# One encoder layer on one Trainium2 core: a new head, another start of the attention, one more early block in each feed-forward product, and sums moved by a turn

## The chip, the cores and the metric

The kernel runs on one core of one Trainium2 chip. The time is the device time of one execution in microseconds (us), lower is better. The core has five engines that are followed here: PE (TensorE: matrix products and transposes), DVE (VectorE), ACT (ScalarE), POOL (GpSimd) and SP (SyncE, which in this kernel only issues DMA transfers; POOL issues most of the others). Each engine works through its own list of instructions in order; between engines there are semaphores.

## The reference, cut to what matters

One layer over a sequence of 1024 rows of 1024 numbers, all in fp32:

```
h = swiglu(rmsnorm(x, ffn1_pre_g), w_gate, w_up, w_down)     # 1024 -> 2816 -> 1024
x = x + 0.5 * rmsnorm(h, ffn1_post_g)
h = rmsnorm(x, mix_pre_g);  q, k, v = h @ w_qkv              # 16 heads of 64
o_na  = neighbourhood_attention(first 8 heads, rel_bias)     # 16 x 64 grid, softmax
o_dil = dilated_mixture(last 8 heads, t5_bias)               # 3 windowed softmaxes, merged
x = x + rmsnorm([rmsnorm(o_na) | rmsnorm(o_dil)] @ w_out, mix_post_g)
x = x + 0.5 * rmsnorm(swiglu(rmsnorm(x, ffn2_pre_g), ...), ffn2_post_g)

rmsnorm(x, g) = x * rsqrt(mean(x*x) + 1e-6) * g
swiglu(x)     = (silu(x @ w_gate) * (x @ w_up)) @ w_down
```

## The kernel before

**Numbers.** Every fp32 operand is split in a high part (ACT: a cast to fp32r, `hi`) and the rest (DVE: a subtraction, `lo`). A product is three matrix products, hi·hi (L268), lo·hi (L269), hi·lo (L270), in one PSUM bank.

**Strassen.** Large products are done with one level of Strassen-Winograd: seven block products instead of eight. The operand (the normalised rows, transposed) exists in seven forms (A11, A12, A22 and sums S1 to S4), the weights too. `PairGemm` does the gate and up projections in 22 blocks of 128 columns: block b takes one 512 KB load of each of the two weight matrices, and seven **chains** of 12 matmuls 128x512, one chain for each form. `run` goes through the blocks: u (L491), v (L499), c22 (L520) and c21 (L528) are the additions on DVE that put the chains together, and c21 belongs to a last chain (A22) that is held back and runs in the next block. A chain that goes on in a bank waits for the addition that reads the bank ahead of it. The weight sums of the next block (L453 to L455) and the splits (L362 on ACT, L363 on DVE) are spread over the block.

**Early blocks.** The operand of a sub-layer is made from rows that arrive in eight tiles of 128 rows. The first four tiles give A11 and A12. So `ahead` runs the A11 and A12 chains of the first `early` blocks before the rest of the operand exists, and keeps their sum in DRAM (L438); `plan` gives each of these turns some steps (norm, transposes of one tile, sums of the operand). In `run`, an early block has five chains and loads its kept sum (L487). Before, there are 9 early blocks in the first feed-forward product (FFN1), 8 in the q/k product, 11 in the second (FFN2). The gated product of a block goes to `sink`: L568 to L587, in which every odd block adds four sums for the pair. Near the end of each gate phase the down projection's weights are summed as well (L333 to L335).

**Head.** The start of the program: two tiles of x are loaded, the norm weights come as a row broadcast to 128 partitions (512 KB, on POOL's queue), ACT squares the rows, DVE makes the root in 12 small operations on 128x2 (L143 to L154), then scales each tile (L217), PE transposes it (L176), ACT and DVE split it (L177, L178). Then the A11 chains of blocks 0 and 1 run by halves of 256 columns. From the first turn of `ahead` on, each block has A11 and A12 chains, and the tiles 4 to 7 are normed and transposed beside them.

**q/k product.** A planned `ahead` of 8 turns, whose turn 0 ends the sums and makes the norm of tiles 6 and 7 and transposes tile 5, then value passes, then `run` over 8 blocks; block 7's last chain ends it. Each block's q and k of one pair of heads are split, written to DRAM by POOL (L893 to L911) and read back as `st`. Two plan entries load the first heads of the attention (`load_head`: g, va and vb, 13 DMAs for the first), at turns 5 and 7.

**Attention, first head.** A head of the dilated group is worked in units of two blocks of 128 queries: scores on PE (L1035), maximum with bias on DVE (L935), exponentials on ACT (L940), four transposes on PE (L946), a copy (L951), values on PE (L1047). The order of units is a small pipeline: PE does the scores of units ahead of the transposes of the one before. The q of the first head is rearranged by residue on ACT (L917, 128x1024), that of later heads on POOL.

Of the kernel before, what the change touches and what calls it, by code (L numbers as in the profile page):

```python
# [19 lines left out]
P, T = 128, 512  # L20
# [319 lines left out]
class PairGemm:  # L340
# [137 lines left out]
    def run(self, final=None):  # L478
# [3 lines left out]
        for b in range(self.n):  # L482
# [48 lines left out]
            c.tick()  # L531
        last()


class GatePairs:
# [7 lines left out]
    def first(self, b, ps, keep, s1=None):  # L543
        c, nc = self.c, self.c.nc
        sg = c.sp.tile([P, T], F32, tag="s1", name="sg") if keep else self.tile()
# [306 lines left out]
class QKPairs:  # L852
# [15 lines left out]
    def last(self, b, q, k):  # L868
        self.put(b, 0, 1, q)
        self.put(b, 1, 1, k)  # L870

    def put(self, b, kind, h, x):
        c, nc = self.c, self.c.nc
        p = QK_ORDER[b]
        e = c.sp.tile([P, 2, T], F32R, tag="qk", name="qk", bufs=c.qkbufs)
# [44 lines left out]
def q_by_residue(c, copy, st):  # L920
    q = c.op.tile([P, SEQ], F32R, tag="q", name="q")
    by_residue(copy, q, st[:, 0])
    return q
# [53 lines left out]
class DilPair:  # L977


    def __init__(self, c, p, then):  # L980

        self.c, self.p, self.pi, self.then = c, p, p - NP, then
# [7 lines left out]
    def outputs(self):  # L990
        c = self.c
        self.oa = c.op.tile([P, 8, VW], F32, tag="oa", name="oa")
        self.sa = c.op.tile([P, 8, 2], F32, tag="sa", name="sa")
        self.ob = c.op.tile([P, 8, RW], F32, tag="ob", name="ob")

    def head(self, hd, st, q, g, late, parts=(1, 0)):
        for part in parts:
            for quad in range(2):
# [6 lines left out]
    def unit(self, hd, st, q, g, part, quad, un, po):  # L1005
# [5 lines left out]
        def scores():  # L1011
            ps = c.pss.tile([P, 2, 256], F32, tag="s", name="sp")
            s = c.pp.tile([P, 2, 256], F32, tag="s", name="s")
            pb = s if part else c.op.tile([P, 2, 256], F32, tag="pb", name="pb", bufs=4)
# [218 lines left out]
def layer(tc, a, out):  # L1233
    nc = tc.nc
    c = Ctx(tc)
    with ExitStack() as ctx:
# [80 lines left out]
        def ffn(which, op, prep, pg, get, turns, sums, more, post, pre, src, dst, begin=None,  # L1317
# [8 lines left out]
            if begin:  # L1326
                left_pool(e)
                pg.start()
# [95 lines left out]
        with ExitStack() as order:  # L1424
# [9 lines left out]
            load((0, 1), (nc.sync, nc.scalar))  # L1434
            op0 = Operand(c, load_gain(c, a["ffn1_pre_g"], "pre"), 0)

            def begin(pg):
                load((2, 3), (nc.scalar, nc.sync))

                def drain():  # L1440
                    while c.sums:
                        c.sums.popleft()()

                def norm(*ts):
                    op0.scale(*n[ts])
                    drain()
                def junk():
                    return c.xp.tile([P, D], F32, tag="s", name="junk", bufs=2)
                n = {(0, 1): op0.squares([0, 1], [xs[0], xs[1]], junk())}
                norm(0, 1)  # L1450
                pg.split_left(0)
                n[2, 3] = op0.squares([2, 3], [xs[2], xs[3]], junk())
                op0.one(0)
                op0.one(1)
                pg.split_left(1)
                acc, s1 = [pg.bank() for _ in range(2)], []
                for b in range(2):
                    pg.mm(acc[b], pg.w[b], 0, A11, cols=slice(0, 256))
                op0.one(0)
                norm(2, 3)  # L1460
                op0.one(2)
                op0.one(3)
                for b in range(2):
                    pg.mm(acc[b], pg.w[b], 0, A11, cols=slice(256, 512))
                    s1.append(pg.save(b, acc[b]))
                    if b:
                        op0.one(1)
                load((4, 5), (nc.gpsimd, nc.gpsimd))
                op0.one(2)
                op0.one(3)  # L1470
# [30 lines left out]
            op, fin, hs, prep = ffn(1, op0, prep, gate_pairs(1, op0, a["wg1"], a["wu1"], 9), get1,  # L1501
# [271 lines left out]
```

## Time and profile before

| | us |
|---|---|
| median of 3 runs | 1900.07 (1899.72 to 1904.05) |
| the profiled execution | 1899.15 |
| its span in the trace | 1897.0 |
| PE busy in the span | 1842.2 (97%) |
| DVE busy | 1316.3 (69%) |
| ACT busy | 794.9 (42%) |
| POOL busy | 320.7 (17%) |

The span is what the trace covers; around it lie 2.15 us that no engine's instruction shows. PE is at work for 97% of the span, so a time is read from this profile by asking where PE stands still, or runs at a lower clock, and what it waits for there. Durations stand in the rows as nanoseconds or microseconds of one instruction; in rows of the timeline the first number is the start in us, the second how long the row's instructions took together, and the bracket says how long the engine was idle before and what released it.

### The profile page before, as it was taken

What the parts mean: (1) busy time and instruction counts of PE and PEld (TensorE: products, weight loads), DVE (VectorE), ACT (ScalarE), POOL (GpSimd) and SP (SyncE); (2) the same over time, 40 slices, a digit from 0 to 9 for tenths busy, and PEclk for the clock granted to TensorE, in tenths of its full rate; (3) what the DMA queues carried; (4) which work ended last, traced back from release to release, by engine and by line L of the source; (5) the groups of instructions that cost most, each with busy time, mean ns of one, the idle gap of its engine ahead of it and who ended that gap; (6) DMA issues with size and microseconds to landing.
All of it is one profiled execution on the core that took longest, in us unless ns stands there. A gap on an engine that the chain in (4) does not pass through costs nothing.

```text
span 1897.0 us, 25061 instructions
## 1 busy us (share of the span) xinstructions
PE 1842.2 (97%) x9044; PEld 1538.3 (81%) x9044; DVE 1316.3 (69%) x2207; ACT 794.9 (42%) x1285; POOL 320.7 (17%) x519
## 2 busy tenths in 40 slices
PE   5999999999999999999999999999999999999997
PEld 4778788888887887888799987877887888888886
DVE  5778777765655977568566775786878777655557
ACT  4522233333444545324477765453222333344342
POOL 1122122211000022222342310121111111110000
PEclk8999999999999999999999999999999999999999
DMA  6655667664986756656974642484456656576563
GB/s 236 219 195 180 219 204 237 234 235 139 348 297 214 273 170 235 234 161 201 314 262 137 219 157 89 165 311 161 159 191 215 223 190 223 197 276 209 195 230 134
DMA packets 162748, 402.52 MB, mean 212 GB/s; under 512 B 17664, under 2 KB 34272, under 8 KB 160576
## 3 DMA queue, kind: packets, MB, share of 16 engines
q1 hardware_dynamic: 113312, 225.67, 35.6%
q0 software_dynamic: 48448, 173.15, 25.7%
q10 hardware_dynamic: 864, 2.10, 0.3%
q8 instruction: 71, 1.16, 0.2%
q14 instruction: 53, 0.43, 0.1%
HBM read 275.89 MB, written 130.03 MB: 214 GB/s over the span
## 4 chain that ended last, share of the span: by engine, by line
PE 84%; DVE 6%; DMA 4%; issue 3%; ACT 2%; POOL 0%; SPq 0%; DVEq 0%; ACTq 0%; POOLq 0%
PE mmp L268 16%; PE mmp L270 16%; PE mmp L269 16%; PE accp L269 8%; PE accp L268 8%; PE accp L270 8%; PE po L1047 3%; PE ptp L946 2%; PE sp L1035 2%; PE trp L176 1%; PE po L1168 1%; PE sp L1155 1%; DMA tsv<-tr 1%; DMA sgd<-sg 1%; DMA gain<-in_ffn_pre_g_dram 0%
## 5 line engine op out<-in xcount | busy, mean ns | idle before, releaser
L268 PE MATMUL mmp<-x,whi 128*128 128x512 f32 (+1 forms) x1432 | 565.8, 395 | 6.5 <-DVE v L499 4.2
L270 PE MATMUL mmp<-x,wlo 128*128 128x512 f32 (+1 forms) x1432 | 561.2, 392 | 1.7 <-DVE wlo L363 1.7
L269 PE MATMUL mmp<-x,whi 128*128 128x512 f32 (+1 forms) x1432 | 560.7, 392 | 0.5 <-DVE x L178 0.2
L268 PEld LDWEIGHTS mmp<-x,whi 128*128 128x128 f32 x1432 | 271.1, 189 | 67.2 <-issue 6.5
L270 PEld LDWEIGHTS mmp<-x,wlo 128*128 128x128 f32 x1432 | 271.0, 189 | 61.0 <-DVE wlo L363 2.4
L269 PEld LDWEIGHTS mmp<-x,whi 128*128 128x128 f32 x1432 | 271.3, 189 | 58.0 <-DVE x L178 1.4
L638 DVE TENSOR_TENSOR pw<-praw,pw 128x1024 fp32r<-128x1024 f32 (+1 forms) x182 | 199.0, 1138 | 124.6 <-ACT pw L637 122.7
L362 ACT CAST whi<-wraw 128x1024 fp32r<-128x1024 f32 x128 | 134.0, 1051 | 325.7 <-PE mmp L269 257.2
L637 ACT CAST pw<-praw 128x1024 fp32r<-128x1024 f32 (+1 forms) x182 | 168.9, 983 | 206.3 <-PE accp L270 158.6
L269 PE MATMUL accp<-pw 128*128 128x512 f32 x600 | 233.7, 390 | 1.0 <-DVE pw L638 1.0
L268 PE MATMUL accp<-pw 128*128 128x512 f32 x600 | 234.3, 391 | 0.0
L270 PE MATMUL accp<-pw 128*128 128x512 f32 x600 | 233.6, 389 | 0.0
L363 DVE TENSOR_TENSOR wlo<-wraw,whi 128x1024 fp32r<-128x1024 f32 x128 | 156.3, 1223 | 22.3 <-ACT whi L362 22.3
L269 PEld LDWEIGHTS accp<-pw 128*128 128x128 f32 x600 | 112.7, 188 | 24.7 <-DVE pw L638 1.9
L268 PEld LDWEIGHTS accp<-pw 128*128 128x128 f32 x600 | 112.6, 188 | 23.7 <-DVE hb L709 0.2
L270 PEld LDWEIGHTS accp<-pw 128*128 128x128 f32 x600 | 112.6, 188 | 23.6
L570 POOL DMA_DIRECT2D g<-sg x44 | 24.1, 548 | 445.0 <-DVE sg L563 291.7
L381 ACT COPY s<-mmp 128x512 f32<-128x512 f32 x52 | 30.5, 586 | 143.0 <-PE mmp L270 135.5
L178 DVE TENSOR_TENSOR x<-trp,x 128x512 fp32r<-128x512 f32 x84 | 57.3, 687 | 38.7 <-ACT x L177 38.6
L528 DVE TENSOR_TENSOR c<-mmp,u 128x512 f32<-128x512 f32 x52 | 35.8, 688 | 66.3 <-PE mmp L270 66.3
L177 ACT CAST x<-trp 128x512 fp32r<-128x512 f32 x84 | 48.8, 586 | 53.1 <-PE trp L176 52.7
L453 DVE TENSOR_TENSOR wraw<-wraw 128x1024 f32<-128x1024 f32 x52 | 63.5, 1221 | 0.8
(246 smaller groups left out, 2742.6 us busy)
## 6 DMA issues: line engine op xcount, KB each, us to landing
praw<-g SPq DMA_DIRECT2D x70, 512.0 KB
wraw<-in_wg_dram SPq DMA_DIRECT2D x44, 512.0 KB
wraw<-in_wu_dram SPq DMA_DIRECT2D x44, 512.0 KB
tr<-in_wd_dram SPq DMA_DIRECT2D x44, 512.0 KB
g<-sg POOLq DMA_DIRECT2D x88, 256.0 KB, 4.4
ts<-tr POOLq DMA_DIRECT2D x22, 1024.0 KB, 4.9
praw<-ts SPq DMA_DIRECT2D x88, 256.0 KB
praw<-in_wd_dram SPq DMA_DIRECT2D x66, 256.0 KB
```

The costliest lines, as they stand in the source:

```text
L177: nc.scalar.copy(hi, ps)
L178: nc.vector.tensor_sub(lo, ps, hi.bitcast(F32))
L268: nc.tensor.matmul(out, ahi, bhi, start=start, stop=False, skip_group_check=go_on)
L269: nc.tensor.matmul(out, ahi, blo, start=False, stop=False, skip_group_check=go_on)
L270: nc.tensor.matmul(out, alo, bhi, start=False, stop=stop, skip_group_check=go_on)
L362: nc.scalar.copy(hi, raw)
L363: nc.vector.tensor_sub(lo, raw, hi.bitcast(F32))
L453: nc.vector.tensor_sub(r[:, 0:2], r[:, 1:3], r[:, 0:2])
L637: nc.scalar.copy(w[side][:, 0, :m], raw[:, :m])
L638: nc.vector.tensor_sub(w[side][:, 1, :m], raw[:, :m], w[side][:, 0, :m].bitcast(F32))
L946: c.nc.tensor.transpose(self.tps[:, j, :], self.probs[:, j * P:(j + 1) * P], c.ident)
L1047: nc.tensor.matmul(po[0][:, un * 2 + j], u.pt[:, 2 * j + t, :], rhs, start=t == 0, stop=t == 1)
```

## The change

1. **Head.** `begin` is written by hand for all engines. The norm weights come as one row of 4 KB and are spread over the partitions by two matmuls with a row of ones (L1480). Tile 0 and 2 are squared on ACT, tile 1 and 3 on DVE. The root is one Sqrt on ACT and five small DVE operations (L1497 to L1501). Tiles are scaled in halves of 512 columns, weights are loaded and split in halves of 256 KB, x2 and x3 change queues. The A11 chains of three blocks, not two, run there, those of block 0 and 1 by halves, and all eight transposes of the halves of the first four tiles stand between them.
2. **Early blocks.** 10 in FFN1 (the tiles 4 to 7 one turn later in the plan, and the norm of 4 and 5 after ACT's work of its turn), 12 in FFN2.
3. **q/k product.** In `ahead`, the sums and the norm of tiles 6 and 7 and the transposes of tile 5 go from turn 0 to turn 1. In `run`, `load_head` comes at turns 4 and 5, the rearranging of the first head's q (now on POOL) and of its bias at turn 6.
4. **Attention.** The scores of the first two units stand ahead of the last chain of the q/k product, in banks of that product's own pool (`ahead=` of `run`, `begin` of the head, `early` of the unit). The last block's second q/k write is held back (`held`) and done between the first units of the attention.

The core of the diff:

```diff
@@ PairGemm.run
-    def run(self, final=None):
+    def run(self, final=None, ahead=None):
...
             c.tick()
+        if ahead:
+            ahead()
         last()
@@ QKPairs
     def last(self, b, q, k):
-        self.put(b, 0, 1, q)
-        self.put(b, 1, 1, k)
-
-    def put(self, b, kind, h, x):
+        es = [self.tile() for _ in range(2)]
+        for kind, x in enumerate((q, k)):
+            put = lambda kind=kind, x=x: self.put(b, kind, 1, x, es[kind])
+            if b == len(QK_ORDER) - 1:
+                self.c.held.append(put)
+            else:
+                put()
@@ DilPair
+    def begin(self, st, g):
+        self.sa = self.c.small.tile([P, 8, 2], F32, tag="sa", name="sa", bufs=1)
+        po = []
+        for un in range(2):
+            self.c.unit(self.unit(0, st, None, g, 0, 0, un, po, True))
...
         def scores():
-            ps = c.pss.tile([P, 2, 256], F32, tag="s", name="sp")
...
+            if early:
+                ps, s, pb = [pool.tile([P, T], F32, tag=t, name="se" + t).rearrange("p (a b) -> p a b", a=2)
+                             for pool, t in ((c.psm, "mm"), (c.sp, "s1"), (c.sp, "v"))]
+            else:
+                ps = c.pss.tile([P, 2, 256], F32, tag="s", name="sp")
@@ the head
+                nc.scalar.dma_start(row[:1, :D], a["ffn1_pre_g"])
+                load((0, 1), (nc.sync, nc.scalar))
+                fetch(0, 0)
+                load((3, 2), (nc.scalar, nc.sync))
+                for b, i in ((1, 0), (2, 0), (0, 1), (1, 1), (2, 1)):
+                    fetch(b, i)
...
+                for g, ps in enumerate(spread):
+                    nc.tensor.matmul(ps, row[:1, D:], row[:1, g * T:g * T + T], start=True, stop=True)
...
+                def root(t):
+                    x = ss[:, t:t + 2]
+                    q, h, y, e = [c.small.tile([P, 4], F32, tag=n, name=n)[:, :2] for n in ("q0", "v", "y", "e")]
+                    nc.scalar.activation(q, x, AF.Sqrt, bias=eps[:, 0:1], scale=1.0 / D)
+                    nc.vector.tensor_scalar(h, x, -0.5 / D, -0.5 * EPS, op0=ALU.mult, op1=ALU.add)
+                    nc.vector.reciprocal(y, q)
+                    nc.vector.tensor_mul(e, y, h)
+                    nc.vector.tensor_mul(e, e, y)
+                    nc.vector.scalar_tensor_tensor(y, e, 1.5, y, op0=ALU.add, op1=ALU.mult)
...
+                square(0)
+                square_here(1)
+                root(0)
+                nc.scalar.copy(op0.gain[:, :T], spread[0])
+                whigh(0, 0)
+                scale(0, 0)
+                scale(1, 0)
+                turn(0, 0)
+                turn(1, 0)
+                square(2)
+                square_here(3)
+                high(0, 0)
...
+                products(0, (0, 1, 2), first)
...
+                products(2, (2,), every)
+                low(3, 1)
...
@@ the plans
-    ... gate_pairs(1, op0, a["wg1"], a["wu1"], 9), get1,
-        {0: [F(4, 5), L(6, 7)], 2: [U(4)], 3: [F(6, 7), U(5)], 5: [U(6)], 6: [U(7)]},
+    ... gate_pairs(1, op0, a["wg1"], a["wu1"], 10), get1,
+        {0: [lambda: c.behind(F(4, 5), ACT), L(6, 7)], 3: [U(4)], 4: [F(6, 7), U(5)], 6: [U(6)], 7: [U(7)]},
-            plan(8, {0: [A(6, 7), U(5)], 3: [U(6)], 5: [U(7)]})
+            plan(8, {1: [A(6, 7), U(5)], 3: [U(6)], 5: [U(7)]})
-            plan(8, {5: [lambda: queued(load_head)], 7: [lambda: queued(load_head), lambda: queued(first_bias)]})
-            pg.run()
+            plan(8, {4: [lambda: queued(load_head)], 5: [lambda: queued(load_head)],
+                     6: [lambda: queued(first_q), lambda: queued(first_bias)]})
+            c.held, qs = [], deque()
+            pg.run(ahead=ahead)
...
-            pg = gate_pairs(3, op, a["wg2"], a["wu2"], 11)
+            pg = gate_pairs(3, op, a["wg2"], a["wu2"], 12)
```

Three places show how instructions move. In these rows a line of the kernel, an operation, what it writes and reads, and its size stand in the order of one engine; the changed kernel's line numbers are some 10 (later 156) higher for the same code.

PE at the start of the program, before (`trp` is the bank of transposes, `mmp` a bank of products, `xn` a scaled tile):

```order
L176 MATMUL trp<-ident,xn 128x128 x8
L268 MATMUL mmp<-x_155,whi 128x256
L269 MATMUL mmp<-x_156,whi 128x256
L270 MATMUL mmp<-x_155,wlo 128x256
L268 MATMUL mmp<-x_155,whi 128x256
L269 MATMUL mmp<-x_156,whi 128x256
```

and now:

```order
L1480 MATMUL mmp<-row 128x512 x2
L1517 MATMUL trp<-ident,xn 128x128 x8
L1542 MATMUL mmp<-x_149,whi 128x256 x4
L1542 MATMUL mmp<-x_150,whi 128x256 x4
L1542 MATMUL mmp<-x_149,wlo 128x256 x4
L1542 MATMUL mmp<-x_149,whi 128x256 x4
L1517 MATMUL trp<-ident,xn 128x128 x4
L1542 MATMUL mmp<-x_150,whi 128x256 x4
L1517 MATMUL trp<-ident,xn 128x128 x4
L1542 MATMUL mmp<-x_149,wlo 128x256 x4
L1542 MATMUL mmp<-x_149,whi 128x256 x4
L1542 MATMUL mmp<-x_150,whi 128x256 x4
```

The two matmuls that spread the norm weights are first; the transposes of tiles 2 and 3 (rows of x4) stand between the products of block 1 instead of behind both blocks' first halves.

SP in the q/k product's run, from the weight load of one block on, before (`wraw` are a block's weights, `s` is its kept sum, `g`, `va` and `vb` belong to a head of the attention):

```order
L355 DMA wraw<-in_wqk_dram 128x2x512
L356 DMA wraw<-in_wqk_dram 128x1024
L487 DMA s_7316<-s1d 128x512
L355 DMA wraw<-in_wqk_dram 128x2x512
L356 DMA wraw<-in_wqk_dram 128x1024
L973 DMA g<-gab_68 128x384
L973 DMA g<-gab_69 128x384
L961 DMA va<-v_88 128x7x130
L961 DMA va<-v_88 128x2x130 x2
L965 DMA vb<-v_88 128x1x130 x8
L973 DMA g<-gab_68 128x384
L973 DMA g<-gab_69 128x384
```

and now:

```order
L355 DMA wraw<-in_wqk_dram 128x2x512
L356 DMA wraw<-in_wqk_dram 128x1024
L983 DMA g<-gab_68 128x384
L983 DMA g<-gab_69 128x384
L971 DMA va<-v_88 128x7x130
L971 DMA va<-v_88 128x2x130 x2
L975 DMA vb<-v_88 128x1x130 x8
L487 DMA s_7355<-s1d 128x512
L355 DMA wraw<-in_wqk_dram 128x2x512
L356 DMA wraw<-in_wqk_dram 128x1024
L983 DMA g<-gab_68 128x384
L983 DMA g<-gab_69 128x384
```

Before, the 13 transfers of the first `load_head` (g, va, vb) stand behind the last block's weights (the second pair of `wraw` rows); now the same 13 stand behind those of the block before, and the last block's kept sum and weights stand behind the 13.

PE at the end of the q/k product, before (`sp` are scores, `ptp` transposes of the probabilities, `po` products with the values):

```order
L269 MATMUL mmp<-x_5409,whi 128x512
L270 MATMUL mmp<-x_5408,wlo 128x512
L1035 MATMUL sp<-st 128x256 x12
L946 MATMUL ptp<-ident,pb 128x128 x4
L1035 MATMUL sp<-st 128x256 x4
L946 MATMUL ptp<-ident,pb 128x128 x4
L1035 MATMUL sp<-st,q 128x256 x4
L1047 MATMUL po<-va,pt 128x65 x4
```

and now (`semm` are scores in a bank of the product's pool):

```order
L269 MATMUL mmp<-x_5431,whi 128x512
L270 MATMUL mmp<-x_5430,wlo 128x512
L1056 MATMUL semm<-st 128x256 x8
L268 MATMUL mmp<-x_5432,whi 128x512
...
L270 MATMUL mmp<-x_5432,wlo 128x512
L1056 MATMUL sp<-st 128x256 x4
L956 MATMUL ptp<-ident,sev 128x128 x4
L1056 MATMUL sp<-st 128x256 x4
L956 MATMUL ptp<-ident,sev 128x128 x4
L1056 MATMUL sp<-st,q 128x256 x4
L1068 MATMUL po<-va,pt 128x65 x4
```

The scores of the first two units (x8) have moved ahead of the last chain of 12 matmuls. On DVE the same place reads before (k, c: the last additions of the product; L890 the split of q and k, L935 the maximum of a unit's block):

```order
L865 TENSOR_TENSOR k<-mmp,u_7331 128x512
L890 TENSOR_TENSOR qk<-k,qk 128x512
L528 TENSOR_TENSOR c_7428<-mmp,u_7331 128x512
L890 TENSOR_TENSOR qk<-c_7389,qk 128x512
L890 TENSOR_TENSOR qk<-qk 128x512
L935 ISA s,sa<-sp,g 128x256
```

and now:

```order
L867 TENSOR_TENSOR k<-mmp,u_7370 128x512
L945 ISA ses_7453,sa<-semm,g 128x256
L945 ISA sa 128x1
L945 ISA ses_7453,sa<-semm,g 128x256
L945 ISA sa 128x1
L900 TENSOR_TENSOR qk<-k,qk 128x512
L945 ISA ses_7462,sa<-semm,g 128x256
L945 ISA sa 128x1
L945 ISA ses_7462,sa<-semm,g 128x256
L945 ISA sa 128x1
L528 TENSOR_TENSOR c_7484<-mmp,u_7370 128x512
L945 ISA s,sa<-sp,g 128x256
```

The maxima of the first two units stand ahead of the last addition of the product (c, L528), and the splits of its result are gone from in front of the third unit.

More of the change, by code (lines that the diff above doesn't have):

```diff
@@ L544, in first @@
         c, nc = self.c, self.c.nc
[L545 removed]
+        sg = s1 if keep and s1 is not None else (c.sp.tile([P, T], F32, tag="s1", name="sg") if keep else self.tile())
         if s1 is not None:
@@ L1433, in layer @@
             xs = {}
-            load((0, 1), (nc.sync, nc.scalar))
-            op0 = Operand(c, load_gain(c, a["ffn1_pre_g"], "pre"), 0)
+            op0 = Operand(c, None, 0)
             def begin(pg):
[L1438 to L1470, printed above, removed]
@@ new lines, in begin, with scale, save, turn @@
+                r = {}
+                def scale(t, g):
+                    sl = slice(g * T, g * T + T)
+                    nc.vector.scalar_tensor_tensor(xn[t][:, sl], xs[t][:, sl], r[t], op0.gain[:, sl],
+                                                   op0=ALU.mult, op1=ALU.mult)
+                def save(*ts):
+                    for t in ts:
+                        nc.gpsimd.dma_start(op0.saved[t], xn[t])
+                def turn(t, g):
+                    got[t, g] = ps = c.pst.tile([P, 4, P], F32, tag="tr", name="trp")
+                    for j in range(4):
+                        nc.tensor.transpose(ps[:, j, :], xn[t][:, g * T + j * P:g * T + j * P + P], c.ident)
@@ new lines, in products @@
+                def products(b, kinds, cols):
+                    if b == len(acc):
+                        acc.append(pg.bank())
+                    for kind in kinds:
+                        w, x = pg.w[b][kind == 2], op0.x[A11][kind == 1]
+                        for k in range(4):
+                            nc.tensor.matmul(acc[b][:, cols], w[:, 0, k * P:k * P + P], x[:, k, cols],
+                                             start=kind == 0 and k == 0, stop=kind == 2 and k == 3)
+                first, second, every = slice(0, 256), slice(256, 512), slice(0, 512)
@@ new lines, in begin @@
+                for t in range(4):
+                    place(t)
+                square(0)
[10 more added lines that the diff above has]
+                high(0, 0)
+                wlow(0, 0)
+                high(1, 0)
+                low(0, 0)
@@ new lines, in begin @@
+                low(1, 0)
+                root(2)
+                whigh(1, 0)
+                products(0, (0, 1, 2), first)
+                scale(2, 0)
+                scale(3, 0)
+                products(1, (0,), first)
+                turn(2, 0)
+                wlow(1, 0)
+                whigh(0, 1)
+                wlow(0, 1)
+                pg.fetch_left(3)
+                products(1, (1,), first)
+                turn(3, 0)
+                products(1, (2,), first)
+                for t in (2, 3):
+                    high(t, 0)
+                    low(t, 0)
@@ new lines, in begin @@
+                products(0, (0, 1, 2), second)
+                whigh(2, 0)
+                nc.vector.tensor_copy(op0.gain[:, T:], spread[1])
+                whigh(1, 1)
+                scale(0, 1)
+                load((4,), (nc.sync,))
+                scale(1, 1)
+                load((5,), (nc.sync,))
+                turn(0, 1)
+                s1.append(pg.save(0, acc[0]))
+                high(0, 1)
+                scale(2, 1)
+                low(0, 1)
+                products(1, (0, 1, 2), second)
@@ new lines, in begin @@
+                turn(1, 1)
+                high(1, 1)
+                scale(3, 1)
+                s1.append(pg.save(1, acc[1]))
+                low(1, 1)
+                wlow(2, 0)
+                products(2, (0,), every)
+                turn(2, 1)
+                high(2, 1)
+                low(2, 1)
+                products(2, (1,), every)
+                turn(3, 1)
+                high(3, 1)
+                products(2, (2,), every)
+                low(3, 1)
+                wlow(1, 1)
```

85 lines of the change are left out of this document (67 added, 18 removed).

## The prediction

> **What bounds the kernel now.** I read the page first, then the chain that ended last, then the waits of PE.
>
> ```profile
> PE 1842.2 (97%) x9044; PEld 1538.3 (81%) x9044; DVE 1316.3 (69%) x2207; ACT 794.9 (42%) x1285; POOL 320.7 (17%) x519
> PE 84%; DVE 6%; DMA 4%; issue 3%; ACT 2%; POOL 0%; SPq 0%; DVEq 0%; ACTq 0%; POOLq 0%
> PE trp L176 <- DVE xn L217: 18.7, 3, 11.9
> PE trp L176 <- DVE x L178: 6.5, 9, 1.3
> PE mmp L268 <- DVE v L499: 4.2, 2, 2.5
> PE sp L1035 <- DVE sa L935: 3.4, 1, 3.4
> PE mmp L270 <- DVE wlo L363: 1.7, 1, 1.7
> PE ptp L946 <- ACT pb L940: 0.8, 1, 0.8
> ```
>
> PE works for 97% of the span and carries 84% of the last chain. The change takes no matmul of weight out, so it can only win what PE loses: 1897.0 − 1842.2 = 54.8 us of idle time, and what PE does at a lower clock. The waits (us in total, times, longest) say where the idle time is: 18.7 us in the head (transposes that wait for scaled tiles), 4.2 in two early blocks (v), 3.4 + 0.8 at the start of the attention, 6.5 in nine clusters of transposes, 1.7 at the q/k begin. The change touches each of these, so the sum goes place by place.
>
> **The head.**
>
> ```profile
> 0.74 0.39 SPq L1432 DMA_DIRECT2D x<-in_x_dram  x1
> 5.35 1.06 ACT L168 ACTIVATE junk<-x 128x1024 f32<-128x1024 f32 x1 [2.40 <-DMA x<-in_x_dram]
> 9.89 0.16 DVE L154 SCALAR_TENSOR_TENSOR y<-e,y 128x2 f32<-128x2 f32 x1
> 9.97 1.05 ACT L168 ACTIVATE junk<-x 128x1024 f32<-128x1024 f32 x1
> 10.46 2.48 DVE L217 SCALAR_TENSOR_TENSOR xn<-x,y,gain 128x1024 f32<-128x1024 f32 x2 [0.41 <-DMA gain<-in_ffn_pre_g_dram]
> 11.89 2.22 PE L176 MATMUL trp<-ident,xn 128*128 128x128 f32 x8 [11.89 <-DVE xn L217]
> 14.79 0.58 PE L268 MATMUL mmp<-x,whi 128*128 128x256 f32 x1 [0.68 <-ACT x L177]
> 20.38 0.41 PE L270 MATMUL mmp<-x,wlo 128*128 128x256 f32 x1
> 27.40 2.28 PE L176 MATMUL trp<-ident,xn 128*128 128x128 f32 x8 [5.89 <-DVE xn L217]
> 34.88 0.29 PE L268 MATMUL mmp<-x,whi 128*128 128x256 f32 x1
> 38.97 0.50 PE L268 MATMUL mmp<-x,whi 128*128 128x512 f32 x1 [0.68 <-ACT x L177]
> L816 PE MATMUL tabp<-oh,t5t x4: 587/589/591, 120.2 to 135.5; 32*8 32x511 f32 x4
> 24.00:27.00 3.00, 0.00 (x0) 0.00 (x0) 2.65 (x11) 0.00 (x0) 0.00 (x0) 0.61 0.64 236
> 30.00:33.00 3.00, 2.50 (x10) 2.21 (x11) 0.69 (x1) 0.30 (x1) 0.33 (x1) 0.50 0.98 255
> ```
>
> The head is over where the whole A12 chain of block 0 begins: 38.97. The scaling at 10.46 waits for the broadcast weights; without that it would wait for the root (9.89 + 0.16). Both go. The row of 4 KB is there before the tile (5.35), and the two spreading matmuls, for which `tabp` is the nearest (0.59 each, 1.2 at half clock), end before the scale needs them. New order: tile 0 squared from 5.35 (1.06 and a read of 0.19), tile 1 beside it on DVE (a 1024-wide DVE operation takes 1.22), so both at about 6.8; one Sqrt and five small operations at 0.2 each (before, twelve, to 10.05) end at about 8.1; two half scales at 0.6 each give the first transposes at about 9, all done by about 10. What is late next is ACT: the square of tile 2, at 9.97 before, stands ahead of the first `high`. With 9.9 + 1.25 + two casts of 0.58, the first product stands at about **12.25** (14.79 before).
>
> From there PE has 48 matmuls of 256 columns, 12 of 512 and 24 transposes. At full clock (0.12, half of the 0.23 that stood between them before; 0.23 for 512 columns; about 0.11) that is 5.7 + 2.7 + 2.7 = 11.1 us, at half clock about 21. DVE has 18 operations of 0.61 and five small ones in the same stretch, 12 us: it keeps up, barely. The clock decides. Before, 24 matmuls of 256 columns from 14.79 to 20.38 went at half rate (0.23 apart); full rate came just when PE had run dry (the idle stretch 24 to 27 has it fall to 0.61), and the second half ran at 0.50 until 34.88, 4.5 us after products began again. If PE has no such gap, full rate comes about 5.5 us after the first product, near 17.8. By then 2.8 of the 11.1 us are done; 8.3 remain, plus 1.4 for two hand-overs of 0.68 as at 14.79: the A12 chain of block 0 at 27.5. Saved: 38.97 − 27.5 = 11.5, and the third block's A11 chain, 12 × 0.228 = 2.7, is done as well: 14.2. Against it, in the turn that follows, DVE has the old root (twelve small operations, 2.4 us) and two full scales (2.48) ahead of the split of a later block's weights, where the new head has used up its lead: about 1.4 us of stall by my count, and I keep 1 more for waits inside the hand-made order. **−12**; ends −6.5 (half clock throughout) and −14.2.
>
> The Trainium skill ("TensorE: Matmul & The Clock Gate", Part 1, The HAM clock gate) has the same picture: free-running windows of about 3.4 us, half rate until one busy window. The same page (Part 4, PE-mode transpose) says that transposes do not count as busy the same way, which speaks against this head, in which transposes stand between the products. The attention's start bears on it, below.
>
> **FFN1, the last early block.**
>
> ```profile
> 207.67 0.69 DVE L491 TENSOR_TENSOR u<-mmp,s 128x512 f32<-128x512 f32 x1 [1.38 <-PE mmp L270]
> 216.63 0.69 DVE L499 TENSOR_TENSOR v<-mmp,u 128x512 f32<-128x512 f32 x1
> 217.47 0.47 PE L268 MATMUL mmp<-x,whi 128*128 128x512 f32 x1 [1.64 <-DVE v L499]
> 1447.10:1459.10 12.00, 11.96 (x18) 1.00 0.63 217
> 1459.27 0.47 PE L268 MATMUL mmp<-x,whi 128*128 128x512 f32 x1 [2.52 <-DVE v L499]
> 1302.34 0.66 PE L176 MATMUL trp<-ident,s 128*128 128x128 f32 x4 [1.34 <-DVE x L178]
> ```
>
> The last early block has to split the next block's third weight half as well, and block 8, being even, does the pair's four sums of block 7: 9.6 us of DVE from u to v, 1.64 more than PE gives it. With 10 early blocks the last is block 9, odd, without pair sums. It has the down projection's sums instead. From the end of the gate product: 1.26 + six at 0.61 + three at 1.15 = 8.4. Block 10 of FFN2 shows the allowance: there DVE is busy for 12.0 us from the same point, and PE waits 2.52, so 9.5 are free. 8.4 fits: **−1.6** (0 to −1.64). The extra early block moves two chains forward and adds a store and a load of 256 KB; no chain is added.
>
> **FFN2.** Now the last early block is 11, odd, 8.4 again. Block 10 loses the 1.15 split and one 0.6 sum from ahead of v: 12.0 − 1.75 = 10.25, 0.75 late instead of 2.52: −1.8. The plan's last turn held 12 transposes in one cluster, of which the 1.34 at 1302.34 came; one more turn parts them: −1.3. Together **−3.1** (0 to −3.9).
>
> **q/k begin.** The sums of tiles 6 and 7 go a turn later in program order, but on DVE and POOL they end up in the same places before the split (wlo) for which PE waits 1.7, and the transposes that wait 1.25 only move behind 24 matmuls. **0**, between −2.95 (both gone) and 0.
>
> **q/k run, SP's queue.** This is where the change adds a wait.
>
> ```profile
> 883.61 0.59 SPq L356 DMA_DIRECT2D wraw<-in_wqk_dram  x1
> 898.35 0.80 SPq L973 DMA_DIRECT2D g<-gab  x2
> 916.25 0.74 SPq L973 DMA_DIRECT2D g<-gab  x1
> 906.03 1.22 DVE L453 TENSOR_TENSOR wraw<-wraw 128x1024 f32<-128x1024 f32 x1
> 912.15 0.68 DVE L499 TENSOR_TENSOR v<-mmp,u 128x512 f32<-128x512 f32 x1
> 913.58 0.69 DVE L520 TENSOR_TENSOR c<-mmp,v 128x512 f32<-128x512 f32 x1 [0.74 <-PE mmp L270]
> ```
>
> The 13 transfers of the first `load_head` hold SP from 898.35 to 916.25, 17.9 us, since each waits for an older one. They stood behind the last block's weights; now they stand behind those of the block before (883.61) and hold back the last block's kept sum and weights: 884.2 + 17.9 = 902.1, issued by 903.5, landed about 4.6 later (as x: 0.74 to 5.35) at 908 to 909, for a weight sum that ran at 906.03. DVE is nearly full there, so v follows, at landing + 6.8 = 914.8 to 915.8, while PE is ready at 913.5: **+2** (0 to +3.3). The rearranging of q on POOL lies beside this.
>
> **Attention's start.**
>
> ```profile
> 929.70 0.39 PE L268 MATMUL mmp<-x,whi 128*128 128x512 f32 x1
> 936.89 1.22 PE L1035 MATMUL sp<-st 128*128 128x256 f32 x4 [3.35 <-DVE sa L935]
> 937.03 1.28 ACT L940 ACT_TABLE_LOAD   x1
> 942.36 0.90 PE L1047 MATMUL po<-va,pt 128*128 128x65 f32 x5
> 938.00:942.00 4.00, 3.23 (x16) 3.01 (x16) 1.55 (x8) 3.92 (x10) 2.30 (x4) 0.50 1.05 389
> 942.00:946.00 4.00, 4.00 (x35) 4.00 (x35) 2.04 (x10) 3.10 (x7) 2.33 (x2) 0.90 1.02 366
> ```
>
> From the last chain's first matmul (929.70) to the first product with the values (942.36) are 12.66 us. PE's work in it is 12 matmuls of 0.228, 20 scores of 0.138 and 8 transposes of about 0.11: 6.4 us. The rest is 3.35 + 0.77 of waits and some 2 us of half clock that follow them (0.50 from 938 to 942). Now the scores of two units run ahead of the last chain; their maxima (0.34 each), the table load (1.28) and the exponentials lie under its 2.73 us, and the third unit's scores wait only for maxima done by then. 12.66 − 6.4 = 6.3 at most; I leave 0.3 for the hand-over: **−6** (−3.3 if waits of 3 us stay). The held q/k write (about 3 us of ACT and DVE) falls into the attention; ACT has a quarter of its time free from 942 on (3.10 of 4.00), and if that cover were gone it would cost up to 1.
>
> The page's rule on transposes can be weighed here. The trace does not agree with it: by it the half clock should have lasted, since between 938.88 and 942.36 PE ran 8 transposes and 8 scores; full rate is back from 942.8 (0.90 over 942 to 946 is 0.8 us at half). So I let transposes count.
>
> **Sum.** −12 − 1.6 − 3.1 + 0 + 2 − 6 = **−20.7**. The profiled execution took 1899.15 (span 1897.0 and 2.15 around it): 1878.5. It lies 0.9 under the median 1900.07, so against the median 1879.4. I say **1879**.
>
> **The rivals.**
> - *A cold head.* The page's rule, as a mechanism of this kernel: transposes between products keep the half rate up to the end of the first three blocks. Then A12 starts at 12.25 + 21 + 1.4 = 34.7 and the head saves 4.3 + 2.7 less some stall, 6.5: 1885. For it speaks that before, products needed 5.6 us and more to get the full rate; against it, 942.8.
> - *The attention's wait is replaced.* DVE's c (L528) and the exponentials on ACT end later than the third unit needs, or the held writes cost 1: 3 us less are gained, 1882. The same holds if the early block's stall stays (the change not doing what it does by the order): 1881 to 1883.
> - *Slower: the last block's weights.* The 13 transfers were timed with less traffic of weights behind them. With a duration D in place of 17.9, the stall is D − 16.4 (884.2 + 1.2 + 4.6 + 6.8 + D − 913.5, rounded). All other terms give −22.7, so it decides from D = 39 us; at D = 45, 2.5 times the measured one, the kernel is at 1906.
>
> **How the numbers follow.** Forecast, 1873 to 1884: 0.60. Cold head, 1882 to 1889: 0.13. Attention or block, 1880 to 1886: 0.14. All better than counted, below 1873: 0.03. Several gains missing, within 0.3% (5.7 us, about what a measurement of this kernel can tell from no change): 0.06. Slower: 0.04. Faster is 0.60 + 0.13 + 0.14 + 0.03 = 0.90. The ends of the terms added give 1871 (−29.0) and 1893.6 (−6.5); the range 1871 to 1890 leaves out the last cases alone.
>
> **What would show it.** Right: first product near 12, no idle stretch of several us before 40, A12 of block 0 near 27.5; no wait for v in FFN1's early blocks; a wait for v of 1 to 3 us in the q/k product's last block; the first `po` some 6.5 us after the last chain begins, at full clock. Wrong: a granted clock of 0.5 beyond 20, a wait of 5 us or more in the q/k run, new waits for splits in the head's first turns.

## The result, and the profile after

| | before | changed |
|---|---|---|
| median, us | 1899.89 (1898.94 to 1904.05, 4 runs) | 1885.63 (1884.22 to 1886.90, 4 runs) |
| ratio | | 0.9922, 95% interval 0.9910 to 0.9934 |
| profiled execution, span | 1899.15, 1897.0 | 1884.22, 1882.5 |
| PE busy | 1842.2 | 1840.9 |

The change is 14.3 us faster. 20.7 were forecast, and the time lies in the range, 6.6 us above the predicted 1879.

The waits of PE in the changed kernel (us in total, times, longest):

```profile
PE mmp L268 <- DVE v L499: 7.3, 3, 5.5
PE trp L1517 <- DVE xn L1507: 4.2, 2, 3.9
PE trp L176 <- DVE x L178: 3.3, 6, 1.1
PE mmp L270 <- DVE wlo L363: 3.0, 2, 1.7
PE mmp L1480 <- DMA row<-in_ffn_pre_g_dram: 2.7, 1, 2.7
PE mmp L268 <- ACT u L381: 2.4, 2, 1.4
```

The head's 18.7 us of waiting for scaled tiles are gone but for some 5; the attention's start is not in the list any more. The first row is new in its size: the wait for v, 4.2 before, is 7.3, and one wait of 5.5 makes most of it. The last row is new altogether.

The head, in the timeline of the changed kernel:

```profile
6.96 1.23 DVE L1486 CUSTOM_DVE_ANT_0 xn<-x 128x1024 f32<-128x1024 f32 x1 [5.96 <-DMA x<-in_x_dram]
10.21 1.06 ACT L168 ACTIVATE junk<-x 128x1024 f32<-128x1024 f32 x1 [0.63 <-DMA x<-in_x_dram]
10.38 1.94 PE L1517 MATMUL trp<-ident,xn 128*128 128x128 f32 x8 [3.91 <-DVE xn L1507]
12.99 0.58 PE L1542 MATMUL mmp<-x,whi 128*128 128x256 f32 x1 [0.67 <-ACT x L1523]
14.92 1.05 PE L1542 MATMUL mmp<-x,wlo 128*128 128x256 f32 x4
16.62 0.95 PE L1517 MATMUL trp<-ident,xn 128*128 128x128 f32 x4
17.33 0.72 PE L1542 MATMUL mmp<-x,whi 128*128 128x256 f32 x4
27.37 0.40 PE L268 MATMUL mmp<-x,whi 128*128 128x512 f32 x1
40.82 0.50 PE L270 MATMUL mmp<-x,wlo 128*128 128x512 f32 x1 [1.33 <-DVE wlo L363]
```

The A12 chain of block 0 begins at 27.37 (27.5 forecast), the first product at 12.99 (12.25), since tile 1 is there at 6.96 only and tile 2 at 10.21. Four matmuls of 256 columns take 1.05 at 14.92 and 0.72 at 17.33; they start 0.21 apart in the first row and 0.12 apart in the second. Full rate came at 17.33, 4.3 us after the first product (17.8 forecast), and the trace's record of the clock begins there. (The granted clock of 1.00 that a window shows ahead of the first record is no measurement: the products at 14.92 go at half rate under it.) Only one group of four transposes, the row at 16.62, stands between the first product and that point. The forecast's new wait in the next turn stands at 40.82, with 1.33.

The last blocks of the q/k product, on DVE and on SP, and the attention's start on PE:

```profile
870.95 4.65 SPq L971 DMA_DIRECT2D va<-v  x3
875.64 6.50 SPq L975 DMA_DIRECT2D vb<-v  x8
882.24 2.19 SPq L487 DMA_DIRECT2D s<-s1d  x1
884.54 0.59 SPq L355 DMA_DIRECT2D wraw<-in_wqk_dram  x1
885.19 2.00 SPq L356 DMA_DIRECT2D wraw<-in_wqk_dram  x1
```

```profile
897.09 1.23 DVE L453 TENSOR_TENSOR wraw<-wraw 128x1024 f32<-128x1024 f32 x1 [5.39 <-DMA wraw<-in_wqk_dram]
898.35 1.24 DVE L454 TENSOR_TENSOR traw<-wraw 128x512 f32<-128x512 f32 x1
...
903.77 0.69 DVE L499 TENSOR_TENSOR v<-mmp,u 128x512 f32<-128x512 f32 x1
```

```profile
904.61 0.77 PE L268 MATMUL mmp<-x,whi 128*128 128x512 f32 x1 [5.48 <-DVE v L499]
...
922.71 1.10 PE L1056 MATMUL semm<-st 128*128 128x256 f32 x8
...
929.06 0.32 PE L1068 MATMUL po<-va,pt 128*128 128x65 f32 x1 [0.24 <-ACT pt L961]
```

The last block's weights, issued by 887.2, are there at 897.1, and v follows 6.7 us later. PE stands still for 5.48 us. From the first early scores to the first product with the values it is then 6.35 us. Before, the same work took 12.66 us, from the last chain's start; some 6.5 were forecast. By windows (us, PE busy and count, granted clock, DMA share, GB/s):

```profile
872.00:876.00 4.00, 4.00 (x19) 1.00 1.02 359
876.00:880.00 4.00, 4.00 (x20) 1.00 1.10 324
880.00:884.00 4.00, 4.00 (x19) 1.00 1.09 382
884.00:888.00 4.00, 4.00 (x19) 1.00 1.01 336
888.00:892.00 4.00, 4.00 (x20) 1.00 1.05 346
892.00:896.00 4.00, 4.00 (x19) 1.00 0.74 260
896.00:900.00 4.00, 3.13 (x14) 1.00 0.10 36
900.00:904.00 4.00, 0.00 (x0) 0.67 0.85 243
904.00:908.00 4.00, 3.39 (x8) 0.50 1.00 380
908.00:912.00 4.00, 4.00 (x18) 0.97 0.43 164
```

Two things are to be seen. All DMA engines are full from 872 to 892 (a DMA share of 1.01 to 1.10), and the last block's weights come 5 us behind the end of that. And the wait costs twice: the clock falls to a half from 901.4 to 908.2, so that PE, at work again at 904.6, loses another 1.8 us (half of 3.6).

In the first feed-forward, block 10 (DVE and PE of the changed kernel):

```profile
231.74 1.23 DVE L333 TENSOR_TENSOR tr<-tr 128x1024 f32<-128x1024 f32 x1 [6.55 <-DMA tr<-in_wd_dram]
...
234.33 0.68 DVE L528 TENSOR_TENSOR c<-mmp,u 128x512 f32<-128x512 f32 x1
...
252.27 1.23 DVE L333 TENSOR_TENSOR tr<-tr 128x1024 f32<-128x1024 f32 x1 [5.11 <-DMA tr<-in_wd_dram]
```

```profile
236.21 0.50 PE L268 MATMUL mmp<-x,whi 128*128 128x512 f32 x1 [1.38 <-ACT u L381]
...
256.74 0.50 PE L268 MATMUL mmp<-x,whi 128*128 128x512 f32 x1 [0.97 <-ACT u L381]
```

The old wait of 1.64 for v in block 8 is gone; in its place DVE waits 6.55 and 5.11 us for the down projection's weights (tr), everything queued behind (c of L528, and ACT's work on it) is late, and PE loses 1.38 and 0.97.

### The profile page after: what moved, and what is told of

It reads as the page before. It is cut to its first block, busy times and chain, and to the rows that moved or that the text cites. A ratio compares the mean times of both kernels' runs of the same rounds, so it can differ in the third digit from the quotient of the medians.

```text
span 1882.5 us, 25100 instructions
## 1 busy us (share of the span) xinstructions
PE 1840.9 (98%) x9048; PEld 1536.6 (82%) x9048; DVE 1318.3 (70%) x2212; ACT 789.3 (42%) x1283; POOL 324.2 (17%) x521
## 4 chain that ended last, share of the span: by engine, by line
PE 56%; issue 27%; DMA 7%; DVE 6%; POOL 3%; ACT 2%; SPq 0%; POOLq 0%; DVEq 0%; ACTq 0%
PE mmp L268 9%; PE mmp L270 9%; PE mmp L269 9%; PE accp L270 6%; PE accp L268 6%; PE accp L269 6%; PE po L1068 3%; DMA tr<-in_wd_dram 2%; PE ptp L956 2%; PE sp L1056 1%; DMA ts<-tr 1%; PE trp L176 1%; PE po L1189 1%; POOL g L591 1%; PE sp L1176 1%
## 5 line engine op out<-in xcount | busy, mean ns | idle before, releaser
L268 PE MATMUL mmp<-x,whi 128*128 128x512 f32 x1412 | 558.8, 396 | 10.0 <-DVE v L499 7.3
L270 PE MATMUL mmp<-x,wlo 128*128 128x512 f32 x1412 | 553.3, 392 | 3.0 <-DVE wlo L363 3.0
L269 PE MATMUL mmp<-x,whi 128*128 128x512 f32 x1412 | 552.6, 391 | 0.2 <-DVE x L1527 0.2
L268 PEld LDWEIGHTS mmp<-x,whi 128*128 128x128 f32 x1412 | 265.6, 188 | 70.6 <-issue 6.2
L270 PEld LDWEIGHTS mmp<-x,wlo 128*128 128x128 f32 x1412 | 265.5, 188 | 63.3 <-DVE wlo L363 4.4
L269 PEld LDWEIGHTS mmp<-x,whi 128*128 128x128 f32 x1412 | 265.8, 188 | 56.2 <-DVE x L1527 0.5
L528 DVE TENSOR_TENSOR c<-mmp,u 128x512 f32<-128x512 f32 x52 | 35.8, 688 | 53.6 <-PE mmp L270 53.6
L178 DVE TENSOR_TENSOR x<-trp,x 128x512 fp32r<-128x512 f32 x76 | 52.0, 688 | 24.9 <-ACT x L177 24.7
L177 ACT CAST x<-trp 128x512 fp32r<-128x512 f32 x76 | 44.5, 587 | 42.6 <-PE trp L176 42.4
```

The costliest lines, as they stand in the source:

```text
L177: nc.scalar.copy(hi, ps)
L178: nc.vector.tensor_sub(lo, ps, hi.bitcast(F32))
L268: nc.tensor.matmul(out, ahi, bhi, start=start, stop=False, skip_group_check=go_on)
L269: nc.tensor.matmul(out, ahi, blo, start=False, stop=False, skip_group_check=go_on)
L270: nc.tensor.matmul(out, alo, bhi, start=False, stop=stop, skip_group_check=go_on)
```

## The experiments

Each is a small edit of the changed kernel. Each ratio is to runs of the kernel before on the same chip; medians from different chips lie some 1 us apart, so waits and positions in the trace are compared first.

**1. load_head at turns 5 and 7 again.**

```diff
-plan(8, {4: [lambda: queued(load_head)], 5: [lambda: queued(load_head)],
-         6: [lambda: queued(first_q), lambda: queued(first_bias)]})
+plan(8, {5: [lambda: queued(load_head)], 6: [lambda: queued(first_q), lambda: queued(first_bias)],
+         7: [lambda: queued(load_head)]})
```

> The changed kernel with load_head at turns 5 and 7 again (the rearranging of q and of the bias stays at turn 6). Theory: the 5.5 us wait for v in the q/k product's last block comes from the transfers of the first load_head, which hold back the last block's weights, and the half clock after it (some 1.8 us of lost work) comes from that wait. Then both go, the attention still starts without a wait, and the time is 7 us below the changed kernel, about 1878.5. Rival: the wait comes with the new start of the attention or the POOL work (q, bias) in that place; then it stays and the time is 1885 to 1886.

Measured: 1885.64 (1880.24 to 1889.02), ratio 0.9920 (0.9894 to 0.9945). The wait of 5.5 us and the half clock behind it are gone, as the theory says. The time is not lower: it is the rival's number, but not by the rival's mechanism, since the wait does not stay. Two other waits have come, for v in the last block and for the second head's st:

```profile
914.26 0.47 PE L268 MATMUL mmp<-x,whi 128*128 128x512 f32 x1 [1.72 <-DVE v L499]
...
933.17 1.20 PE L1056 MATMUL sp<-st,q 128*128 128x256 f32 x4 [2.92 <-DMA st<-qk]
```

Behind the second the clock is at a half until 938.8, which costs PE another 2.8 us. So 1.72 + 2.92 + 2.8 = 7.4 us have come for the 7.3 (5.48 + 1.8) that went. The first of them is seen on DVE and POOL of this run:

```profile
908.01 1.83 DVE L363 TENSOR_TENSOR wlo<-wraw,whi 128x1024 fp32r<-128x1024 f32 x1 [0.17 <-ACT whi L362]
909.76 2.49 DVE L900 TENSOR_TENSOR qk<-c,qk 128x512 fp32r<-128x512 f32 x1
912.18 1.34 DVE L900 TENSOR_TENSOR qk<-qk 128x512 fp32r<-128x512 f32 x1
```

```profile
907.88 0.88 POOL L927 COPY g<-g 128x384 f32<-128x384 f32 x1 [8.34 <-DMA g<-gab]
...
909.28 2.42 POOL L927 CAST q<-st 128x1024 fp32r<-128x1024 f32 x1
```

An L900 takes 0.69 elsewhere; beside POOL's copies it takes 2.49 and 1.34. In the second wait the second head's st is late, asked for only at turn 7. So load_head at turn 4 paid for an early second head with the last block's weights.

**2. The weight sums of the first feed-forward one turn later.**

```diff
-one_a_turn(sums, NF, NF - 3 + (which == 3) - len(sums), tables(pool, bt))
+one_a_turn(sums, NF, NF - 2 - len(sums), tables(pool, bt))
```

> The changed kernel with the down projection's weight sums of the first feed-forward one turn later (so that the first of them falls into block 10, no early block, as before the change). Theory: the two waits of 1.4 and 1.0 us in blocks 10 and 11 come from the loop store, load, sum, which takes about 20 us and now begins in an early block of some 14 us. Then both waits go and the time is about 2.3 us lower, 1883.3. Rival: the waits come from the blocks' own DVE work; then they stay, 1885.6.

Measured: 1884.17 (1880.97 to 1885.27), ratio 0.9913 (0.9898 to 0.9929). Both waits are gone from the trace (no wait of PE above 0.3 us between 79 and 695); before the next phase PE stands 2.8 us earlier (695.45 for 698.25). The loop is shown as the cause of the two waits. A lower time is not shown: the difference, 1.5 us, is within its interval, and in this trace part of the 2.8 goes again in a wait of 1.87 at 714, with 3.4 us of half clock behind it, and one of 1.05 at 978.

**3. The scores behind the last chain, the writes still held.**

```diff
-pg.run(ahead=ahead)
+pg.run()
+ahead()
```

> The changed kernel with the first two units' scores behind the last chain of the q/k product again, all else as changed (the writes of the last block still held). Theory: moving the scores ahead is worth what the attention's start cost before, 4.1 us of waits and about 2.6 of half clock; the half clock is there already in the changed kernel, so here the waits for maxima and exponentials come back, 3 to 5 us, and the time is 1889 to 1891. Rival: holding the last block's writes back is what helped, not the order of the scores; then the time stays within 1 us of the changed kernel.

Measured: 1887.4 (1884.49 to 1890.62), ratio 0.9934 (0.9913 to 0.9954). The theory falls: only 0.53 us of waits come back where 3 to 5 were expected (the time is too near the changed kernel's to decide), and from the last chain's first matmul (921.70) to the first product with the values (928.72) are 7.02 us, 0.67 more than in the changed kernel. The writes are tried next.

**4. The last block's writes not held, the scores ahead.**

```diff
-if b == len(QK_ORDER) - 1:
+if b == len(QK_ORDER):
     self.c.held.append(put)
```

> The changed kernel with the scores of two units ahead of the last chain, but the last block's second q/k write done at once, as before, ahead of the third unit's maxima on DVE and ahead of the attention's copies on ACT. After the run with the scores behind the chain lost only 0.5 us of waits, the theory is that holding the writes back is the larger part of the new start: then 2 to 4 us of waits come back between the third unit's scores and the first product with the values. Rival (the prediction's reading): the scores' place is the larger part; then under 1 us comes back.

Measured: 1886.61 (1886.24 to 1888.44), ratio 0.9935 (0.9920 to 0.9950). PE in this run:

```profile
928.20 0.71 PE L1056 MATMUL sp<-st 128*128 128x256 f32 x4
...
931.78 0.71 PE L1056 MATMUL sp<-st,q 128*128 128x256 f32 x4 [2.43 <-DVE sa L945]
932.75 0.44 PE L1068 MATMUL po<-va,pt 128*128 128x65 f32 x2 [0.26 <-ACT pt L961]
```

The third unit's maxima stand behind the two splits on DVE; from the first scores (923.71) to the first product with the values are 9.04 us, 2.7 more than in the changed kernel. Against the 12.66 of before, holding the writes without the scores' move (experiment 3) wins 5.6, the scores' move without holding 3.6, both 6.3. The copy of q, 2.04 us on ACT before and now on POOL, is in both runs; it was not tried alone.

**5. vb issued by POOL.**

```diff
-c.nc.sync.dma_start(vb[:, ci, j], ...
+(c.nc.gpsimd if n == 1 else c.nc.sync).dma_start(vb[:, ci, j], ...
```

> The changed kernel with the eight vb transfers of the first load_head issued by POOL, on its own queue, in place of SP (turns 4 and 5 unchanged). Theory A: the last block's weights are late because they stand behind the 13 transfers on SP's queue; then SP issues them some 6 us earlier, they land near 888 (897 in the changed kernel), and the 5.5 us wait for v goes. Theory B: they are late because all the DMA engines are full with the head's transfers from 872 to 892; then they land at 893 to 896 whoever issues vb, and 3 us or more of the wait stay.

Measured, one execution: 1885.95. PE still waits 3.50. SP of this run, which stands 3.1 us later than the changed kernel at this place (the weights of the block before at 871.68 for 868.61):

```profile
881.16 0.33 SPq L487 DMA_DIRECT2D s<-s1d  x1
885.48 0.56 SPq L355 DMA_DIRECT2D wraw<-in_wqk_dram  x1
886.09 0.59 SPq L356 DMA_DIRECT2D wraw<-in_wqk_dram  x1
```

SP is free well before, and issues the weights in their old rhythm (13.8 us after the block before); the sum that needs them still begins at 897.06 (894.0 on the changed kernel's clock), 11 us after the issue. The DMA share is 1.00 or more from 876 to 904. By its own sign (3 us or more of the wait stay) that is theory B. The shorter queue is worth 3.1 us at the sum and 2.0 at PE (3.50 for 5.48); the rest of the wait stays with SP on time and the DMA engines full. Which of the transfers then under way holds the weights up was not tried.

**6. The head of before.** (`begin` of the kernel before, in the changed kernel.)

> The changed kernel with the head of before (weights broadcast, two blocks, root in 12 operations). Theory: the head is worth 11.6 us at the A12 chain of block 0, plus 2.7 for the third block's chain, less 1.3 of a new wait: the time is about 13 us higher, 1898.5. Rival: part of that is given back later in the first feed-forward (DMA, DVE): 8 to 10 us higher.

Measured: 1896.8 (1893.17 to 1902.17, 10 runs), ratio 0.9984 (0.9970 to 0.9997). 0.9984 − 0.9922 of 1900 is 11.8 us, between the two expectations; by the two intervals it is uncertain by some 3.4 us, so neither is ruled out. The head is the larger part of the change's gain. The head's A12 chain begins at 40.23 in this trace (after a wait that ends 39.55 + 0.68), 12.9 later than in the changed kernel.

**7. 9 and 11 early blocks.**

```diff
-gate_pairs(1, op0, a["wg1"], a["wu1"], 10)
+gate_pairs(1, op0, a["wg1"], a["wu1"], 9)
...
-gate_pairs(3, op, a["wg2"], a["wu2"], 12)
+gate_pairs(3, op, a["wg2"], a["wu2"], 11)
```

> The changed kernel with 9 and 11 early blocks again (the plan of turns as changed). Theory: in the first feed-forward the two waits of the sums' loop (1.4 and 1.0 us) go and the old wait for v (1.6) comes back; in the second the wait of 2.5 in block 10 and a cluster wait of about 1.3 come back in place of 0.8 and 1.0. Together the time is within 2 us of the changed kernel; the waits are to be read in the trace. Rival (the prediction's sum): 1.6 and 3.1 us higher, 4 to 5 us in all.

Measured, one execution: 1895.79, above both expectations. The waits came as the theory has them (1.64 in the first feed-forward, 1.07 and 2.52 in the second); but the plan of turns is the changed one, with one turn less to stand on, so that the transposes wait 1.06 + 0.80 + 0.55 near 75, and the clock is at a half from 75.3 for 6.8 us and again for 3.4 us behind the wait of 2.52. Those two stretches explain at most 5 us; the rest of the 10 was not followed, so this run does not price the early blocks.

**8. The q/k begin at turn 0.**

```diff
-plan(8, {1: [A(6, 7), U(5)], 3: [U(6)], 5: [U(7)]})
+plan(8, {0: [A(6, 7), U(5)], 3: [U(6)], 5: [U(7)]})
```

> The changed kernel with the sums and the norm of tiles 6 and 7 and the transposes of tile 5 at turn 0 of the q/k product's ahead again. Theory (the prediction's): the wait for the weights' split, 1.7 us near 703, is the same with and without the move, and the waits of transposes around it sum up alike within 1 us. Rival: the move took 1 us or more off these waits, which come back.

Measured, one execution: 1883.37. The waits there are 0.54 and 1.70; with the move, 0.76, 1.70 and 0.29. The wait for the split is the same, as the theory says; the move is worth nothing that shows.

**9. Both heads at turn 5, and the sums one turn later.**

```diff
-plan(8, {4: [lambda: queued(load_head)], 5: [lambda: queued(load_head)],
+plan(8, {5: [lambda: queued(load_head), lambda: queued(load_head)],
          6: [lambda: queued(first_q), lambda: queued(first_bias)]})
...
-one_a_turn(sums, NF, NF - 3 + (which == 3) - len(sums), tables(pool, bt))
+one_a_turn(sums, NF, NF - 2 - len(sums), tables(pool, bt))
```

> The changed kernel with the weight sums one turn later, both load_head at turn 5, q and bias at turn 6. Theory: with load_head at 5 the last block's weights go ahead of the transfers, so no wait for v above 1 us in the block before the last; the second head's st is asked for early, so the 2.9 us wait for it at 930 (heads at 5 and 7) goes; what stays is up to 1.7 us in the last block, where POOL's copy of q slows DVE. 1878 to 1881. Rival: the traffic only moves, and another wait of 3 us or more shows up; then 1883 to 1886.

Measured: 1876.54 (1873.28 to 1879.17), ratio 0.9884 (0.9865 to 0.9904). The waits of PE in this run:

```profile
PE trp L176 <- DVE x L178: 4.6, 6, 1.1
PE trp L1517 <- DVE xn L1507: 4.5, 2, 4.2
PE mmp L270 <- DVE wlo L363: 3.0, 2, 1.7
...
PE mmp L268 <- DVE v L499: 0.8, 1, 0.8
```

The wait for v is 0.8 (7.3 in the changed kernel, and that 0.8 is FFN2's block 10), neither the 1.7 of experiment 1 nor its 2.9 is there, and the clock is never at a half between the head and the end. POOL's copies of q and of the bias run from 903.7 to 906.6 here, where DVE mostly waits for PE, so no L900 stands beside them. The time is below the expected 1878 to 1881. Two things are changed at once; their shares were not measured apart, but experiment 2 has one of them alone.

**10. Heads at 5 and 6, q at 7.**

```diff
+plan(8, {5: [lambda: queued(load_head)], 6: [lambda: queued(load_head)],
+         7: [lambda: queued(first_q), lambda: queued(first_bias)]})
```

(with the sums one turn later)

> The changed kernel with the weight sums one turn later, load_head at turns 5 and 6, q and bias at turn 7. Theory: as both heads at 5, and POOL's copy of q now falls under the last chain and the first units, where DVE has slack: no wait of 1.7 us in the last block, but DVE's maxima there are drawn out, up to 1 us of waits at the attention's start. 1877 to 1880. Rival: q comes too late for the fifth unit's scores, 2 us or more of waits there; then above 1881.

Measured: 1878.4 (1877.69 to 1879.68), ratio 0.9890 (0.9876 to 0.9905). No wait in the last block; 3.07 us at the third unit's scores, where the maxima (DVE sa L945) come late, and 3.4 us of half clock. That is more wait than the expected 1, within the expected time.

**11 and 12. The changed kernel and experiment 9 on one chip.**

> The changed kernel itself once more, for the comparison with the next one on the same chip: 1884 to 1887, with the wait of 5.5 us for v near 899 and half clock behind it.

> The kernel with both load_head at turn 5 and the weight sums one turn later, once more: 1875 to 1879, 7 to 10 us under the changed kernel on this chip, with no wait of PE above 2 us after 40 us. If its first result was a matter of the chip, the two lie within 5 us.

Measured: the changed kernel 1886.55 (1885.91 to 1889.73), ratio 0.9932 (0.9918 to 0.9945); both heads at 5 1875.52 (1874.74 to 1877.93), ratio 0.9873 (0.9860 to 0.9887). The second is 11.0 us under the changed kernel (7 to 10 were expected), with intervals that do not meet; the longest wait of PE behind 40 us is 1.7. It is faster than both kernels.

## Why the prediction was right or wrong

The terms, each as forecast and as the traces of before and after have it:

| term | forecast | measured |
|---|---|---|
| head | −12 | −13.0 (38.97 − 27.37 = 11.6, the third chain 2.7, less 1.33) |
| FFN1, last early block | −1.6 | +0.7 (1.64 gone, 1.38 + 0.97 new) |
| FFN2 | −3.1 | −2.0 (1.34 + 2.52 gone, 0.79 + 1.04 stay) |
| q/k begin | 0 | −0.2 |
| q/k run, SP's queue | +2 | +7.3 (5.48 of wait, 1.8 of half clock) |
| attention's start | −6 | −6.3 |

- **The head** was right in size and in its steps. The first product came 0.7 late and the full rate 0.5 early (17.33 for 17.8), and the two nearly cancel. That the full rate came so near its forecast is in part luck: in the 12 traces with the new head it comes between 16.2 and 19.2, 3.1 to 6.2 us after the first product, and block 0's A12 chain between 26.9 and 28.2. The cold head did not come, but its mechanism was hardly put to the test: in the 3.4 us ahead of the full rate PE had products and, in the last 0.7 us, four transposes. So the Trainium skill's sentence on transposes ("TensorE: Matmul & The Clock Gate", Part 4, PE-mode transpose) had no effect on the time here, and that transposes count is not shown. The attention's start of before doesn't show it either, as the prediction had it: there too scores stand among the transposes.
- **The early block of FFN1** failed in its step "8.4 fits". The DVE sum is right, but the down projection's sums were counted as ready work. They are a loop: store, load, sum, 20.3 and 20.5 us from one L333 to the next (211.47, 231.74, 252.27), and with 10 early blocks the first stands in an early block, which is over in some 14. Experiment 2 shows it. The wait for v that was to go did go; what is new is a wait for u.
- **The q/k run** is the term that was mis-sized, and it alone is 5 us of the 6.6 missing. The mechanism, 13 transfers ahead of the last block's weights, was right. SP was done even earlier than reckoned: the transfers held it for 12.1 us, not 17.9, and the weights were issued by 887.2, where 889.1 was forecast (903.5, less the 14.4 us by which this kernel is ahead at this place). What failed is "landed about 4.6 later (as x)": the price of a load at the program's start was used for one that stands behind a stretch with full DMA engines, where it is 10 us (887.2 to 897.1). Experiment 1 shows that the early transfers are the cause, experiment 5 that the full engines are a part of it. The rival that priced this place varied the wrong quantity, how long the transfers hold SP (and its terms add up to D − 16.7, not D − 16.4, on which nothing hangs). And of the prediction's own signs of being wrong one came here: a wait of 5 us or more in the q/k run. The half clock behind the wait was not in the sum at all, though the same trace had shown it at the attention's start.
- **The attention's start** was right in total, and its reason only half. The prediction gave the gain to the scores' place; by experiments 3 and 4 it adds 0.7 to what the held writes win, and these add 2.7 to what it wins. The prediction had priced the held writes only as a cost.
- **The q/k begin** was right: nothing (experiment 8).
- **FFN2**: block 10 as forecast (0.79 for 0.75); block 11 waits 1.04, where none was forecast, since its DVE list too begins with an L333 that waits for its load (2.07 us in this run). In the 12 traces with 12 early blocks the two go together: DVE waits 0.70 to 2.77 us there, and PE 1.0 less, or not at all. That is the same slip as in FFN1.
- The rest: some 1.2 us went in the attention at 1085.7, where the clock is at a half for 3.4 us without a new wait; other runs have it elsewhere or not at all. With the small waits of before at 53 to 59 (0.7) and 574 to 577 (1.05), which the changed kernel's trace doesn't have, the terms come to −14.1; the spans differ by 14.5. Each term is read from one trace of each kernel, and places the change does not touch differ by some tenths of a microsecond, up to 1 or 2 us, between traces.

## What to carry to other kernels

A step that is moved earlier takes its transfers with it: price what then stands behind them by a landing time from a stretch with the same DMA load, not from an idle one, and move such loads behind the last weights of a phase if they have time. When work is moved into shorter turns, look for loops through DRAM beside it, whose period does not shrink. And a wait of PE is worth more than its length: behind the head, each wait of 2.9 us and more in these traces is followed by half clock that costs another 1.7 to 3.0 us. Of four waits of 2.4 to 2.5 us, two cost nothing more.

## What the runs showed of the hardware

- DVE is slowed by POOL's copies: a 128x512 operation that takes 0.69 us took 2.49 beside a POOL cast of 128x1024 (2.42), 1.34 beside a POOL copy of 128x384 (1.32), and 1.24 beside another such copy in the changed kernel. In experiment 1 the two L900 end 0.55 us behind POOL's two copies (912.25 for 911.70, 913.52 for 912.96), as if they had stood still until POOL was done. The Trainium skill ("SBUF — State Buffer", SBUF: two separate sides) says just that: the pair of ports that the two engines share is locked for a whole instruction, not split, against DVE operations with two inputs in SBUF. The trace agrees.
- The clock fell to a half some 2 us into an idle stretch of 5.5 us (899.1 to 904.6, half from 901.4 on) and stayed there for 6.83 us, 3.6 of them with PE at work. In all 14 traces each stretch of half clock between the start and the last 20 us lasts 3.41, 6.83, 10.24 or 13.65 us, whole multiples of 3.41. So the same wait can cost more or less: in six traces with this wait, of 5.4 to 5.6 us, the half clock behind it cost PE between 1.8 and 3.0 us.
- With the DMA engines full, the last 512 KB load of a block was in use 9.9 us after SP had issued it (887.2 to 897.1), and 10.4 us after in experiment 5 (886.7 to 897.1). At the program's start a tile of the same size took 4.6.
